# A SwiGLU layer on one core: one weight sum by an accumulating transfer, and six of seven products of 17 blocks with hi and lo side by side

## The chip, the core and the metric

The kernel runs on one core of a Trainium2 chip. The metric is the device time of one execution in microseconds (us). A core has a matrix engine (PE), whose weight loads appear in the profile as a lane of their own (PEld), a vector engine (DVE), a scalar engine (ACT), a general engine (POOL) and a queue engine (SP). Each works through its own list of instructions, and they wait for each other by semaphores. Transfers are issued by SP and POOL here and carried by 16 DMA engines.

## What is computed

The reference is one layer of a decoder with three sublayers and a final norm. The change touches only the first matrix product of the third one:

```python
    hf = rms_norm(x, norm_ffn[l])
    gate, up = jnp.split(hf @ w_ffn_in[l], 2, axis=-1)
    x = x + (jax.nn.silu(gate) * up) @ w_ffn_out[l]
return rms_norm(x, norm_final)
```

`hf` is 512 x 1024, `w_ffn_in` 1024 x 5632 (2816 gate columns and 2816 up columns), all in float32.

## The kernel before

**Precision.** Every float32 operand is held as two reduced-precision tiles, hi (a cast, on ACT) and lo (the operand minus hi, on DVE). A product is then hi x hi + hi x lo + lo x hi, three matmuls.

**The gate and up products.** The 2816 hidden columns are worked in 22 blocks m of 128. For one block the two products (gate and up) on two halves of the tokens and two halves of the contraction are formed by a seven-product scheme: seven weight forms, seven token forms, products 0 to 6, each over four steps k of the contraction with 256 tokens. The four raw weight quarters of a block lie in HBM next to each other. What is made of them:

- `ws`: two sums, each by a plain load followed by an accumulating load from POOL (L862). It gives the forms of products 4 and 2 ("pair 1").
- `wg`: quarters 0 and 1. It gives forms 0 and 1 ("pair 0"). Then `sum_third` (L874, DVE) adds one of the sums into the first half of `wg`, which gives form 3 (`third_cast`).
- `a` (the "corner", its own buffer): quarter 3 is loaded into its first half by `load_corner` (L868, SP), and `sum_last` (L878, DVE) writes the sum of the two halves of `wg` into its second half. It gives forms 5 and 6 ("pair 2").

`pair_cast` casts 128x1024 on ACT (L887); `rest_of` subtracts on DVE (L1006). For the form of product 3 both are 128x512 (L895, L1006).

**Narrow and wide products.** Where the token form keeps hi and lo side by side in one tile, one matmul of 512 columns does hi x (hi, lo), and a second of 256 columns does lo x hi (L909, L917): "wide". Else there are three matmuls of 256 (L914): "narrow". Products 1, 2 and 6 are wide in all blocks, product 5 in blocks 5 to 18 (`WIDE`), products 0, 3 and 4 never. A wide product leaves its result in two halves of a PSUM bank that still have to be added.

**Reading the banks.** Products 0, 3, 4 and 5 of a block add up in one bank z, which is copied out after 0, 3 and 4 (ACT, L946, 128x256) before the next one adds to it. `joined_halves` (L936, L937) adds both halves of a wide bank to such a copy, in two DVE instructions of 128x256: for product 1, for product 2 (`second`) and for product 6. `evict` then multiplies the gate half by the norm factors (L960), applies silu on ACT (L962), and forms the hidden activations (L971 where product 5 is wide, L974, L974, and L978 in every second block).

**Order.** PE, ACT and DVE follow the program's order. In the steady part the products run as (m,3), (m,2), (m,4), (m+1,0), (m+1,1), (m,5), (m,6), and the table `todo` says after which product each cast, subtraction, sum and read is put on its engine. p and q in that table are the positions of the products of m and m+1. Of each named piece of work, the part on the reads comes first, then the pieces in the order of the calls of `at`. The order on SP and POOL is made by the scheduler.

Of the kernel before, what the change touches and what calls it, by code (L numbers as in the profile page):

```python
# [11 lines left out]
ALU = mybir.AluOpType  # L12
# [13 lines left out]
NF = HID // P  # L26
HS = S // 2
# [17 lines left out]
def hybrid_layer(ctx: ExitStack, tc: tile.TileContext, xT_d, memT_d, mem_d, cols_d, wv_d, win_d,  # L45
                 wbr_d, wmix_d, wmq_d, wmk_d, wmv_d, wmo_d, wfi_d, wfo_d, gfin_d, out):
    nc = tc.nc
# [16 lines left out]
    def nm(s):  # L64
        count[0] += 1
        return f"{s}{count[0]}"
# [4 lines left out]
    def tmp(s, cols=512):  # L71
        return tpool.tile([P, cols], F32, tag="t", name=nm(s), padded_shape=[P, 512])

    def f(ap):
        return ap.bitcast(F32)
# [160 lines left out]
    first = nc.scalar.dma_start(gcol, cols_d)  # L236
# [398 lines left out]
    for m in range(KD):  # L635
        sig = []
        for j in range(2):
            if (m, j) not in gates:
                gate(m, j)
            t = gates.pop((m, j))  # L640
# [20 lines left out]
    for m in range(KD):  # L661
# [9 lines left out]
        t = tmp("km", MEM)  # L671
# [27 lines left out]
    def forms_of(xe, xo):  # L699

        b11, b12, b21, b22 = xe[:, :HS], xe[:, HS:], xo[:, :HS], xo[:, HS:]
        c, d = f(unit("c1")), f(unit("c2"))
        n1, t3, n2, t4 = c[:, :HS], c[:, HS:], d[:, :HS], d[:, HS:]
        nc.vector.tensor_tensor(out=n1, in0=b11, in1=b12, op=ALU.subtract)
        nc.vector.tensor_tensor(out=t3, in0=b22, in1=b12, op=ALU.subtract)
        nc.vector.scalar_tensor_tensor(out=n2, in0=n1, scalar=-1.0, in1=b22, op0=ALU.mult,  # L708
                                       op1=ALU.subtract)
        nc.vector.scalar_tensor_tensor(out=t4, in0=n2, scalar=-1.0, in1=b21, op0=ALU.mult,  # L710
                                       op1=ALU.subtract)
        u = unit("xf")
        nc.scalar.copy(u[:, :HS], b11)
        nc.vector.tensor_tensor(out=u[:, HS:], in0=b11, in1=f(u[:, :HS]), op=ALU.subtract)
        a, b = slice(0, HS), slice(HS, S)

        def beside(src, s):
            both = unit(s)
            nc.scalar.copy(both[:, a], src)
            nc.vector.tensor_tensor(out=both[:, b], in0=src, in1=f(both[:, a]), op=ALU.subtract)  # L720
            return both[:, a], both[:, b], both

        first = beside(b21, "xo")
        second, fourth = beside(n1, "xc"), beside(t3, "xc")
        third, fifth = beside(n2, "xd"), beside(t4, "xd")
        last = beside(b22, "xo")
        return [(u[:, a], u[:, b]), first, second, third[:2], fourth[:2], fifth, last]

    def residual(w_dram, act, old, gain, pairs=False):

# [56 lines left out]
    for h in range(MH):  # L787
        q = q_next
        scs = []
        for t2 in range(2):  # L790
            ps = ztile("sc")
            scs.append(ps)
            for i in range(2):
                t = 2 * t2 + i
# [5 lines left out]
        for t2 in range(2):  # L800
# [6 lines left out]
                                           in1=r1s[:, 2 * t2:2 * t2 + 2], op0=ALU.mult,  # L807
# [3 lines left out]
            for i in range(2):  # L811
                t = 2 * t2 + i
# [5 lines left out]
            for i in range(2):  # L818
                nc.vector.tensor_scalar(out=pr[:, i * MEM:(i + 1) * MEM],
                                        in0=pr[:, i * MEM:(i + 1) * MEM],  # L820
# [22 lines left out]

    KP = KD // 2
    raws, corners = {}, {}

    def ffn_load(m):

# [15 lines left out]

    def load_corner(m):

        a22 = corners[m] = fpool.tile([P, 2, 512], F32, tag="w2", name=nm("a22"))
        i = nc.sync.dma_start(a22[:, 0, :], wfi_d[m][:, 3 * 512:])  # L868
        if m < 2:
            after(i, [loads[-6]])  # L870

    def sum_third(m, eng=nc.vector):
        wg, s13 = raws[m]
        eng.tensor_tensor(out=wg[:, 0, :], in0=s13[:, 1, :], in1=wg[:, 0, :], op=ALU.add)  # L874

    def sum_last(m, eng=nc.vector):
        wg = raws[m][0]
        eng.tensor_tensor(out=corners[m][:, 1, :], in0=wg[:, 0, :], in1=wg[:, 1, :], op=ALU.add)  # L878

    wforms = {}  # L880

    def pair_cast(m, which):

        raw = (*raws[m], corners[m])[which]
        hi = wpool.tile([P, 2, 512], F32R, tag="wh", name=nm("wf"))
        lo = wpool.tile([P, 2, 512], F32R, tag="wl", name=nm("wf"))
        nc.scalar.copy(hi, raw)  # L887
        for n, i in enumerate(((0, 1), (4, 2), (5, 6))[which]):
            wforms[m, i] = hi[:, n, :], lo[:, n, :]
        return raw, hi, lo  # L890
# [11 lines left out]
    def product(ps, m, i, ks=range(KP)):  # L902

        rests = []
        for k in ks:
            hi, lo = (w[:, k * P:(k + 1) * P] for w in wforms[m, i])
            xh, xl, *both = x2f[k][i]
            if both and (i != 5 or m in WIDE):
                nc.tensor.matmul(ps, hi, both[0], start=i < 3 and k == 0, stop=False,  # L909
                                 skip_group_check=True)  # L910
                rests.append((ps[:, :HS], lo, xh))
                continue
            for j, (a, b) in enumerate(((hi, xh), (hi, xl), (lo, xh))):
                nc.tensor.matmul(ps[:, :HS], a, b, start=i < 3 and k == 0 and j == 0,  # L914
                                 stop=k == KP - 1 and j == 2, skip_group_check=True)
        for operands in rests:
            nc.tensor.matmul(*operands, start=False,  # L917
                             stop=ks[-1] == KP - 1 and operands is rests[-1],
                             skip_group_check=True)

    WIDE = range(5, NF - 3)
    banks, silus = {}, []
    acts = {}

# [10 lines left out]
    def joined_halves(out_, bank, old):  # L935
        nc.vector.tensor_tensor(out=out_, in0=bank[:, :HS], in1=old, op=ALU.add)  # L936
        nc.vector.tensor_tensor(out=out_, in0=bank[:, HS:], in1=out_, op=ALU.add)  # L937

    def reads(m, i):

        b = banks[m]
        z, s, t = b["z"][:, :HS], b["s"], b["t"]
        if i == 5 and m in WIDE:
            nc.scalar.copy(s[:, :HS], b["z"][:, HS:])
        elif i in (0, 3, 4):
            nc.scalar.copy((s[:, :HS], None, None, s[:, HS:], t[:, :HS])[i], z)  # L946
        elif i == 1:
            joined_halves(b["g"][:, :HS], b["v"], s[:, :HS])
        elif i == 6:
            joined_halves(b["g"][:, HS:], b["y"], s[:, HS:])  # L950

    def second(m):
        b = banks[m]
        joined_halves(b["t"][:, HS:], b["y"], b["t"][:, :HS])

    def evict(m, part):
        b = banks[m]
        g = b["g"]
        if part == 0:
            nc.vector.tensor_tensor(out=g, in0=g, in1=r2b[0], op=ALU.mult)  # L960
        elif part == 1:
            silus.append(nc.scalar.activation(g, g, AF.Silu))  # L962
        else:
            j, odd = divmod(m, 2)
            if not odd:
                acts[j] = f(unit("a1")), f(unit("a2"))
            to = slice(odd * HS, (odd + 1) * HS)
            first = b["z"][:, :HS]
            if m in WIDE:
                first = b["s"][:, :HS]  # L970
                nc.vector.tensor_tensor(out=first, in0=b["z"][:, :HS], in1=first, op=ALU.add)  # L971
            for half, u in enumerate((first, b["t"][:, HS:])):
                sl = slice(half * HS, (half + 1) * HS)
                nc.vector.scalar_tensor_tensor(out=acts[j][half][:, to], in0=u, scalar=-1.0,  # L974
                                               in1=g[:, sl], op0=ALU.mult, op1=ALU.mult)
            if not odd:
                n1 = acts[j][1][:, :HS]
                nc.vector.tensor_tensor(out=n1, in0=acts[j][0][:, :HS], in1=n1, op=ALU.subtract)  # L978
# [5 lines left out]
    m = NF - 1  # L984
# [134 lines left out]
    def at(n, *some):  # L1119
        todo.setdefault(n, []).extend(some)  # L1120

    def made(n, cast, *args, late=1):

        parts = []
        at(n, lambda: parts.append(cast(*args)))
        at(n + late, lambda: rest_of(*parts[0]))
# [14 lines left out]
    for m in range(1, NF - 1):  # L1141
        p = {i: uses.index((m, i)) for i in range(2, 7)}
        q = {i: uses.index((m + 1, i)) for i in range(2)}
        if m > 1:
            at(p[3], lambda m=m: sum_third(m + 1))
            at(p[3], lambda m=m: evict(m - 1, 0))
            at(p[2], lambda m=m: evict(m - 1, 1))
            at(q[0], lambda m=m: evict(m - 1, 2))
            made(p[3], pair_cast, m, 2)
            made(p[2], third_cast, m + 1)  # L1150
        else:
            made(p[4], third_cast, m + 1)
        at(p[4], lambda m=m: second(m))
        if m + 2 < NF:
            at(p[4], lambda m=m: load_corner(m + 2))
        made(q[0], pair_cast, m + 1, 1, late=2)
        at(q[1] if m < NF - 2 else p[4], lambda m=m: sum_last(m + 1))
        if m + 2 < NF:
            made(p[5], pair_cast, m + 2, 0)
    at(uses.index((0, 4)), lambda: second(0))  # L1160
# [33 lines left out]
    with tc.manual_schedule(engines={mybir.EngineType.PE, mybir.EngineType.Activation,  # L1194
# [69 lines left out]
        last = NJ - 2, NJ - 1  # L1264
# [17 lines left out]
        u = [plus("u", res[3][s2], s0[s2]) for s2 in range(2)]  # L1282
# [252 lines left out]
```

## Time and profile before

| | us |
|---|---|
| median of 3 runs | 839.92 (839.05 to 839.99) |
| the profiled execution, its own time | 838.75 |
| its span, first to last instruction | 837.0 |
| PE busy | 828.8 |
| VectorE busy | 684.6 |
| ScalarE busy | 463.9 |
| GpSimd busy | 161.2 |

The gate and up products stand from about 530 to 721 us of the span, and the down projection follows. Busy times are of single engines and overlap. A row of the timeline has the start in us, the time it took in us, the engine, the line, the operation and the tiles (written <- read). An instruction's start to the next one's start can be shorter than the time it took, since the end of one overlaps the start of the next. "x12" means that 12 like instructions in a row are merged. "[0.62 <-DVE fg L960]" says that the engine stood idle for 0.62 us before it and what ended that.

### The profile page before, as it was taken

What the parts mean: (1) busy time and instruction counts of PE and PEld (TensorE: products, weight loads), DVE (VectorE), ACT (ScalarE), POOL (GpSimd) and SP (SyncE); (2) the same over time, 40 slices, a digit from 0 to 9 for tenths busy, and PEclk for the clock granted to TensorE, in tenths of its full rate; (3) what the DMA queues carried; (4) which work ended last, traced back from release to release, by engine and by line L of the source; (5) the groups of instructions that cost most, each with busy time, mean ns of one, the idle gap of its engine ahead of it and who ended that gap; (6) DMA issues with size and microseconds to landing.
All of it is one profiled execution on the core that took longest, in us unless ns stands there. A gap on an engine that the chain in (4) does not pass through costs nothing.

```text
span 837.0 us, 11962 instructions
## 1 busy us (share of the span) xinstructions
PE 828.8 (99%) x4374; PEld 714.1 (85%) x4374; DVE 684.6 (82%) x1086; ACT 463.9 (55%) x796; POOL 161.2 (19%) x168
## 2 busy tenths in 40 slices
PE   9999999999999999999999999999999999999996
PEld 7888888888888888888888789999999999888885
DVE  7879899996756576587555698999999999999886
ACT  7567868674332355434444566645555555576654
POOL 0011131110566630173000031111111110000401
PEclk9999999999999999999999999999999999999999
DMA  8552435235687865566431326677767673465552
GB/s 303 155 166 101 122 111 103 74 115 174 228 312 276 304 249 188 182 233 249 148 82 51 101 51 161 167 184 200 197 180 197 176 184 95 170 213 197 180 183 101
DMA packets 51357, 143.69 MB, mean 172 GB/s; under 512 B 5761, under 2 KB 7041, under 8 KB 48482
## 3 DMA queue, kind: packets, MB, share of 16 engines
q1 hardware_dynamic: 41650, 107.89, 38.2%
q0 software_dynamic: 9360, 34.75, 15.8%
q8 instruction: 34, 0.56, 0.3%
q10 hardware_dynamic: 288, 0.28, 0.1%
q14 instruction: 25, 0.20, 0.1%
HBM read 125.20 MB, written 13.64 MB: 166 GB/s over the span
## 4 chain that ended last, share of the span: by engine, by line
PE 99%; DVE 0%; ACT 0%; DVEq 0%; issue 0%
PE z L914 13%; PE p L1228 12%; PE pr L161 8%; PE pr L162 8%; PE pr L163 8%; PE y L909 5%; PE r L162 3%; PE r L163 3%; PE r L161 3%; PE v L288 3%; PE y L917 2%; PE v L909 2%; PE km L666 2%; PE mq L163 2%; PE mq L161 2%; PE mq L162 2%
## 5 line engine op out<-in xcount | busy, mean ns | idle before, releaser
L156 ACT CAST wh<-wr 128x1024 fp32r<-128x1024 f32 x84 | 88.0, 1051 | 144.2 <-issue 80.0
L157 DVE TENSOR_TENSOR wl<-wr,wh 128x1024 fp32r<-128x1024 f32 x84 | 111.0, 1321 | 32.0 <-ACT wh L156 31.9
L161 PE MATMUL pr<-xgh,wh 128*128 128x512 f32 x288 | 112.8, 392 | 0.0
L162 PE MATMUL pr<-xgl,wh 128*128 128x512 f32 x288 | 112.4, 390 | 0.0
L163 PE MATMUL pr<-xgh,wl 128*128 128x512 f32 x288 | 112.3, 390 | 0.0
L611 POOL TENSOR_TENSOR pre<-pre 128x512 f32<-128x512 f32 x44 | 70.9, 1616 | 31.5 <-DMA pre<-in_w_ffn_out_dram 29.2
L862 POOL DMA_DIRECT2D ws<-in_w_ffn_in_dram x22 | 26.6, 1209 | 248.5 <-DVE c L708 54.0
L163 PEld LDWEIGHTS pr<-xgh,wl 128*128 128x128 f32 x288 | 54.1, 188 | 11.5
L161 PEld LDWEIGHTS pr<-xgh,wh 128*128 128x128 f32 x288 | 54.1, 188 | 10.6
L162 PEld LDWEIGHTS pr<-xgl,wh 128*128 128x128 f32 x288 | 54.1, 188 | 10.5
L914 PE MATMUL z<-xd,wf 128*128 128x256 f32 x360 | 47.5, 282 | 0.0
L946 ACT COPY sa<-z 128x256 f32<-128x256 f32 x44 | 16.4, 373 | 51.9 <-PE z L914 51.9
L914 PEld LDWEIGHTS z<-xd,wf 128*128 128x128 f32 x360 | 45.0, 190 | 0.1
L1006 DVE TENSOR_TENSOR wf<-wg,wf 128x1024 fp32r<-128x1024 f32 (+1 forms) x44 | 43.1, 978 | 1.5
L1006 DVE TENSOR_TENSOR wl<-wr,wh 128x1024 fp32r<-128x1024 f32 x33 | 41.0, 1242 | 1.8 <-ACT wh L1073 1.8
L1073 ACT CAST wh<-wr 128x1024 fp32r<-128x1024 f32 x33 | 34.5, 1050 | 5.3 <-ACT f01h L1002 2.6
L914 PE MATMUL z<-xf,wf 128*128 128x256 f32 x264 | 35.4, 283 | 0.0
L914 PE MATMUL z<-xc,wf 128*128 128x256 f32 x264 | 35.1, 283 | 0.0
L914 PEld LDWEIGHTS z<-xf,wf 128*128 128x128 f32 x264 | 33.4, 192 | 0.1
L914 PEld LDWEIGHTS z<-xc,wf 128*128 128x128 f32 x264 | 33.0, 190 | 0.0
L368 DVE TENSOR_TENSOR g<-pr,r0b 128x512 f32<-128x512 f32 x16 | 11.0, 687 | 23.5 <-PE pr L163 23.5
L417 POOL TENSOR_SCALAR_AFFINE_SELECT e<-e 128x128 f32<-128x128 f32 (+1 forms) x24 | 10.7, 447 | 86.6 <-DVE e L470 86.6
(356 smaller groups left out, 2239.9 us busy)
## 6 DMA issues: line engine op xcount, KB each, us to landing
wr<-in_w_in_dram SPq DMA_DIRECT2D x36, 512.0 KB, 3.4
pre<-in_w_ffn_out_dram POOLq DMA_DIRECT2D x11, 1024.0 KB, 8.0
sums<-pre POOLq DMA_DIRECT2D x11, 1024.0 KB, 5.0
ws<-in_w_ffn_in_dram SPq DMA_DIRECT2D x22, 512.0 KB, 4.8
wg<-in_w_ffn_in_dram SPq DMA_DIRECT2D x22, 512.0 KB, 4.7
ws<-in_w_ffn_in_dram POOLq DMA_DIRECT2D x22, 512.0 KB, 5.7
wr<-sums SPq DMA_DIRECT2D x22, 512.0 KB, 4.0
wr<-in_w_ffn_out_dram SPq DMA_DIRECT2D x16, 512.0 KB, 3.7
```

Source lines behind the costliest of these rows:

```text
L156: after(nc.scalar.copy(h2, raw), lead[-1:])
L157: lows.append(nc.vector.tensor_tensor(out=l2, in0=raw, in1=f(h2), op=ALU.subtract))
L161: nc.tensor.matmul(ps, a[0], b[0], start=start, stop=False, **kw)
L162: nc.tensor.matmul(ps, a[0], b[1], start=False, stop=False, **kw)
L163: nc.tensor.matmul(ps, a[1], b[0], start=False, stop=stop, **kw)
L611: nc.gpsimd.tensor_tensor(out=t[:, a, :], in0=t[:, a, :], in1=t[:, b, :], op=ALU.add)
L862: nc.gpsimd.dma_start(s13, a[:, 0:4:3, :], accum_op=ALU.add)
L909: nc.tensor.matmul(ps, hi, both[0], start=i < 3 and k == 0, stop=False, skip_group_check=True)
L914: nc.tensor.matmul(ps[:, :HS], a, b, start=i < 3 and k == 0 and j == 0, stop=k == KP - 1 and j == 2, skip_group_check=True)
L1006: nc.vector.tensor_tensor(out=lo, in0=src, in1=f(hi), op=ALU.subtract)
L1073: nc.scalar.copy(hi, raw)
L1228: nc.tensor.matmul(res[i][s2], a[:, ts], b, start=j == 0 and n == 0, stop=n == 2 and j == (BEHIND - 1 if (i, s2) == (5, 1) else NJ - 1))
```

## The change

Two ranges are set: `OWN` (blocks 3 to 20) for the weight sum, `WIDE` (now blocks 3 to 19) for the form of the products.

In the blocks of `OWN` the sum of the two halves of `wg` is made in place by an accumulating transfer from POOL (SBUF to SBUF) in place of the DVE instruction. Quarter 3 is then loaded over the first half of `wg` once form 3 has been cast and subtracted from it, and pair 2 is cast from `wg`. Its cast moves from after product 3 to after product 4, and its subtraction from after product 2 to after product (m+1,0).

In the blocks of `WIDE` products 3 and 4 become wide beside 5. The bank z is then copied whole (128x512) after 3 and 4. `folded` takes the place of `joined_halves` for products 2 and 6: one addition of 128x512 from PSUM, and one of 128x256 that adds the halves in SBUF.

```diff
+    OWN = range(3, NF - 1)
...
     def load_corner(m):
 
+        if m in OWN:
+            nc.sync.dma_start(raws[m][0][:, 0, :], wfi_d[m][:, 3 * 512:])
+            return
...
     def sum_last(m, eng=nc.vector):
         wg = raws[m][0]
+        if m in OWN:
+            nc.gpsimd.dma_start(wg[:, 1, :], wg[:, 0, :], accum_op=ALU.add)
+            return
         eng.tensor_tensor(out=corners[m][:, 1, :], in0=wg[:, 0, :], in1=wg[:, 1, :], op=ALU.add)
...
-        raw = (*raws[m], corners[m])[which]
+        raw = (*raws[m], raws[m][0] if m in OWN else corners[m])[which]
...
-            if both and (i != 5 or m in WIDE):
+            if both and (i not in (3, 4, 5) or m in WIDE):
...
-    WIDE = range(5, NF - 3)
+    WIDE = range(3, NF - 2)
...
-        if i == 5 and m in WIDE:
-            nc.scalar.copy(s[:, :HS], b["z"][:, HS:])
+        if m in WIDE and i in (3, 4):
+            nc.scalar.copy((s, t)[i - 3], b["z"])
+        elif m in WIDE and i == 5:
+            nc.scalar.copy(t[:, :HS], b["z"][:, HS:])
+        elif m in WIDE and i == 6:
+            folded(b["g"][:, HS:], b["y"], s)
...
+    def folded(out_, bank, old):
+        nc.vector.tensor_tensor(out=old, in0=bank, in1=old, op=ALU.add)
+        nc.vector.tensor_tensor(out=out_, in0=old[:, :HS], in1=old[:, HS:], op=ALU.add)
+
     def second(m):
         b = banks[m]
+        if m in WIDE:
+            folded(b["t"][:, HS:], b["y"], b["t"])
+            return
...
             if m in WIDE:
-                first = b["s"][:, :HS]
+                first = b["t"][:, :HS]
...
             at(p[3], lambda m=m: sum_third(m + 1))
+            if m + 1 in OWN:
+                at(p[3], lambda m=m: sum_last(m + 1))
+                at(p[5], lambda m=m: load_corner(m + 1))
             at(p[3], lambda m=m: evict(m - 1, 0))
...
-            made(p[3], pair_cast, m, 2)
+            made(p[4] if m in OWN else p[3], pair_cast, m, 2)
             made(p[2], third_cast, m + 1)
...
-        if m + 2 < NF:
+        if m + 2 < NF and m + 2 not in OWN:
             at(p[4], lambda m=m: load_corner(m + 2))
         made(q[0], pair_cast, m + 1, 1, late=2)
-        at(q[1] if m < NF - 2 else p[4], lambda m=m: sum_last(m + 1))
+        if m + 1 not in OWN:
+            at(q[1] if m < NF - 2 else p[4], lambda m=m: sum_last(m + 1))
```

The token forms of products 3 and 4 are now handed over with their joint tile as well (`third`, `fourth` in place of `third[:2]`, `fourth[:2]`).

Three places show how the instructions now stand. The first is VectorE in one steady block, from the read of the bank of product 6 to the first read of the next product 1. fg is the gate result, sa and sb are copies of the bank z, wf a hi or lo weight tile, a the corner (and, at L974, the activations). Before:

```order
L936 TENSOR_TENSOR fg_6062<-y_6121,sa_6040 128x256
L937 TENSOR_TENSOR fg_6062<-y_6121,fg_6062 128x256
L1006 TENSOR_TENSOR wf_6206<-wg_6075,wf_6205 128x1024
L874 TENSOR_TENSOR wg_6075<-ws_6073,wg_6075 128x512
L960 TENSOR_TENSOR fg_6062<-fg_6062,r0b_4940 128x512
L1006 TENSOR_TENSOR wf_6235<-a_6037,wf_6234 128x1024
L1006 TENSOR_TENSOR wf_6248<-wg_6075,wf_6248 128x512
L936 TENSOR_TENSOR sb_6154<-y_6237,sb_6154 128x256
L937 TENSOR_TENSOR sb_6154<-y_6237,sb_6154 128x256
L971 TENSOR_TENSOR sa_6040<-z_6039,sa_6040 128x256
```

The same place on VectorE in the changed kernel (L1024 is its subtraction, L964 and L965 are `folded`, L878 is `sum_third`, L978 the factor, L989 and L992 the eviction):

```order
L964 TENSOR_TENSOR sa_6064<-y_6143,sa_6064 128x512
L965 TENSOR_TENSOR fg_6090<-sa_6064 128x256
L1024 TENSOR_TENSOR wf_6222<-wg_6103,wf_6221 128x1024
L878 TENSOR_TENSOR wg_6103<-ws_6101,wg_6103 128x512
L978 TENSOR_TENSOR fg_6090<-fg_6090,r0b_4940 128x512
L1024 TENSOR_TENSOR wf_6257<-wg_6103,wf_6257 128x512
L964 TENSOR_TENSOR sb_6172<-y_6247,sb_6172 128x512
L965 TENSOR_TENSOR sb_6172<-sb_6172 128x256
L989 TENSOR_TENSOR sb_6065<-z_6063,sb_6065 128x256
```

The subtraction of pair 2 (128x1024, from a) no longer stands between the factor and the subtraction of form 3 (128x512, from wg); it comes behind the eviction.

The second place is ScalarE in a steady block, from the copy after product 3 to the copy after product 4. Before:

```order
L946 COPY sa_5811<-z_5810 128x256
L887 CAST wf_5889<-a_5692 128x1024
L962 ACTIVATE fg_5720<-fg_5720 128x512
L895 CAST wf_5903<-wg_5733 128x512
L946 COPY sb_5812<-z_5810 128x256
```

ScalarE in the changed kernel, from the copy after product 3 on:

```order
L951 COPY sa_5853<-z_5852 128x512
L980 ACTIVATE fg_5772<-fg_5772 128x512
L902 CAST wf_5942<-wg_5785 128x512
L951 COPY sb_5854<-z_5852 128x512
L894 CAST wf_5953<-wg_5681 128x1024
```

The cast of pair 2 (128x1024) moved from ahead of the silu to behind the copy after product 4; silu, cast of form 3 and that copy keep their order.

The third place is the SP queue in the steady part. Before, each corner has a buffer of its own:

```order
L857 DMA wg_6075<-in_w_ffn_in_dram 128x1024
L853 DMA ws_6073<-in_w_ffn_in_dram 128x2x512
L868 DMA a_6037<-in_w_ffn_in_dram 128x512
L857 DMA wg_6191<-in_w_ffn_in_dram 128x1024
L853 DMA ws_6189<-in_w_ffn_in_dram 128x2x512
```

SP in the changed kernel, where L869 is the load of the corner over the first half of `wg`:

```order
L869 DMA wg_5892<-in_w_ffn_in_dram 128x512
L858 DMA wg_6103<-in_w_ffn_in_dram 128x1024
L854 DMA ws_6205<-in_w_ffn_in_dram 128x2x512
L869 DMA wg_5996<-in_w_ffn_in_dram 128x512
L858 DMA wg_6207<-in_w_ffn_in_dram 128x1024
```

The corner's load now stands ahead of the load of the next `wg`, and on POOL one accumulating transfer of `wg` (L883) stands between each two of `ws` (L863).

More of the change, by code (lines that the diff above doesn't have):

```diff
@@ L726, in forms_of @@
         last = beside(b22, "xo")
-        return [(u[:, a], u[:, b]), first, second, third[:2], fourth[:2], fifth, last]
+        return [(u[:, a], u[:, b]), first, second, third, fourth, fifth, last]
     def residual(w_dram, act, old, gain, pairs=False):
```

## Prediction

> **What bounds the kernel now.** I read the page's busy times, the chain that ended last, and who PE waited for.
>
> ```profile
> PE 828.8 (99%) x4374; PEld 714.1 (85%) x4374; DVE 684.6 (82%) x1086; ACT 463.9 (55%) x796; POOL 161.2 (19%) x168
> PE 99%; DVE 0%; ACT 0%; DVEq 0%; issue 0%
> PE warm L248 <- DVE neg L92: 1.4, 1, 1.4
> ```
>
> PE is the whole chain, and its one wait of 1.4 us is at the start. So any instruction taken from PE shortens the end, as long as nothing else becomes late. Then busy time in a stretch of the gate and up products, where the change lies:
>
> ```profile
> core 0: us, PE busy (x) PEld busy (x) DVE busy (x) ACT busy (x) POOL busy (x), PEclk, DMA share, GB/s
> 610.00:620.00 10.00, 10.00 (x71) 9.30 (x71) 9.69 (x17) 5.49 (x10) 1.20 (x1) 1.00 0.71 185
> ```
>
> VectorE is at 9.69 of 10 us. The page's 82% hides this: here VectorE is almost as full as PE, so its order of work decides whether PE is fed. The chain in order of time prices the products (start, us, what):
>
> ```profile
> 612.23 0.93 PE z L909 x4
> 613.16 0.48 PE z L917 x4
> 613.63 0.93 PE y L909 x4
> 614.57 0.47 PE y L917 x4
> 615.03 1.43 PE z L914 x12
> ...
> 617.87 2.87 PE z L914 x24
> ...
> 622.14 0.93 PE z L909 x4
> ```
>
> A narrow product is 2.87/2 = 1.435 us, a wide one 0.93 + 0.48 = 1.41. From product 5 of one block (612.23) to product 5 of the next (622.14) is 9.91 us: one block.
>
> Last, the timeline of block 11, which holds every term of what follows.
>
> ```profile
> 613.78 1.22 DVE L1006 TENSOR_TENSOR wf<-ws,wf 128x1024 fp32r<-128x1024 f32 x1
> ...
> 614.87 1.59 PE L914 MATMUL z<-xd,wf 128*128 128x256 f32 x12
> 615.07 0.42 DVE L936 TENSOR_TENSOR fg<-y,sa 128x256 f32<-128x256 f32 x1
> ...
> 615.53 0.42 DVE L937 TENSOR_TENSOR fg<-y,fg 128x256 f32<-128x256 f32 x1
> 615.87 1.22 DVE L1006 TENSOR_TENSOR wf<-wg,wf 128x1024 fp32r<-128x1024 f32 x1
> ...
> 617.12 0.70 DVE L874 TENSOR_TENSOR wg<-ws,wg 128x512 f32<-128x512 f32 x1
> ...
> 617.73 0.69 DVE L960 TENSOR_TENSOR fg<-fg,r0b 128x512 f32<-128x512 f32 x1
> 618.33 1.22 DVE L1006 TENSOR_TENSOR wf<-a,wf 128x1024 fp32r<-128x1024 f32 x1
> 618.45 0.64 ACT L962 ACTIVATE fg<-fg 128x512 f32<-128x512 f32 x1 [0.62 <-DVE fg L960]
> 618.99 0.60 ACT L895 CAST wf<-wg 128x512 fp32r<-128x512 f32 x1
> ...
> 619.63 0.69 DVE L1006 TENSOR_TENSOR wf<-wg,wf 128x512 fp32r<-128x512 f32 x1
> 620.24 0.42 DVE L936 TENSOR_TENSOR sb<-y,sb 128x256 f32<-128x256 f32 x1
> ...
> 621.03 0.41 DVE L971 TENSOR_TENSOR sa<-z,sa 128x256 f32<-128x256 f32 x1
> 621.47 0.42 DVE L974 SCALAR_TENSOR_TENSOR a<-sa,fg 128x256 f32<-128x256 f32 x1
> 621.82 0.42 DVE L974 SCALAR_TENSOR_TENSOR a<-sb,fg 128x256 f32<-128x256 f32 x1
> 622.27 0.42 DVE L978 TENSOR_TENSOR a<-a,a 128x256 f32<-128x256 f32 x1
> 622.61 0.42 DVE L936 TENSOR_TENSOR fg<-v,sa 128x256 f32<-128x256 f32 x1
> ...
> 622.91 0.64 PE L917 MATMUL z<-xd,wf 128*128 128x256 f32 x4
> 623.40 0.68 DVE L878 TENSOR_TENSOR a<-wg 128x512 f32<-128x512 f32 x1
> 624.00 1.22 DVE L1006 TENSOR_TENSOR wf<-ws,wf 128x1024 fp32r<-128x1024 f32 x1
> ```
>
> The reader should see a latency that is covered. The factor (L960, 617.73) releases the silu (618.45). Behind the silu on ScalarE stands the cast of form 3 (618.99), and VectorE's subtraction of form 3 waits for that cast (619.63). From L960 to that subtraction it is 1.90 us, of which L960 itself holds VectorE for 0.60 (617.73 to 618.33). The other 1.30 us are filled by the subtraction of pair 2 (618.33).
>
> **The change part by part.**
>
> *PE.* 34 products (3 and 4 in 17 blocks) and product 5 in three more blocks become wide: 37 x (1.435 - 1.41) = 0.9 us less, where PE stays the bound.
>
> *Read-outs on VectorE.* `folded` is one addition of 128x512 with a PSUM source, then one of 128x256. The nearest row with a PSUM source:
>
> ```profile
> L368 DVE TENSOR_TENSOR g<-pr,r0b 128x512 f32<-128x512 f32 x16 | 11.0, 687 | 23.5 <-PE pr L163 23.5
> ```
>
> It takes 0.69 us, and a dependent instruction starts some 0.03 later (615.87 + 1.22 = 617.09 against 617.12): 0.72, then 0.34 (615.53 to 615.87), together 1.06. Now the pair takes 0.80 (615.07 to 615.87). So each of the two read-outs costs 0.26 more. The bounds for the 128x512 are 0.60 (start to start where nothing depends, 617.73 to 618.33) and 0.75; I take 0.72, since the second addition does depend.
>
> [...] L936 and L937 with a PSUM source and L978 with none all take 0.42 us. [...]
>
> *`sum_last` off VectorE.* 0.60 us per block saved (623.40 to 624.00). With two read-outs at +0.26, VectorE's pure work stays about level: -0.08.
>
> *Pair 2 moved, the term that decides.* Its subtraction goes behind the eviction. Nothing takes its place after the factor, and the queue is worked in order, so VectorE stands still for the 1.30 us between L960's slot and the cast of form 3, in every block. That is more than all its slack. How little that is, an earlier block shows, where VectorE ran 0.2 us behind PE:
>
> ```profile
> 604.18 1.22 DVE L1006 TENSOR_TENSOR wf<-ws,wf 128x1024 fp32r<-128x1024 f32 x1
> ...
> 605.31 0.42 DVE L936 TENSOR_TENSOR fg<-y,sa 128x256 f32<-128x256 f32 x1
> ```
>
> Here the subtraction holds VectorE for 1.13 us. In block 11 it would have been free at 613.78 + 1.13 = 614.91, and it read product 6 at 615.07: 0.16 us of slack. What is late next is pair 2's lo. Product 5 needs it at its second half (622.91); now it is done at 618.33 + 1.22 = 619.55, 3.36 us ahead. After the change it comes behind the read-out of product 2 and the eviction, and PE waits for it. Queued behind the waiting subtraction on VectorE are `second`, the eviction, pair 2, product 1's read-out, pair 1.
>
> The loop, from VectorE's first read of product 6 to the next one:
>
> - read-out 1.06; pair 0 1.25 (615.87 to 617.12); `sum_third` 0.61
> - factor to form 3, now bare: 1.90; form 3 0.61 (619.63 to 620.24)
> - `second` 1.06; eviction 621.03 to 622.61 1.58 with L978 (odd blocks), 0.45 less without
> - pair 2's subtraction to its end 1.22, and 0.03 to PE
> - second half of product 5 0.48, product 6 0.93 + 0.47, and 0.20 to VectorE (614.87 to 615.07)
>
> The sum is 11.40 us in odd blocks and 10.95 in even ones, against 9.91 now. VectorE's own stream alone, with pair 2 at 1.13, product 1's read-out 0.79 (622.61 to 623.40) and pair 1 1.14 in place of the last two lines, gives 11.14 and 10.69: the path through PE is the longer one, but both exceed the 9.86 (9.91 - 2 x 0.025) that PE needs.
>
> Blocks 3 to 19: 9 x 11.40 + 8 x 10.95 = 190.2, less 0.26 and 0.45 in block 3, whose first read-out and eviction belong to the narrow block 2: 189.5. Before, 17 x 9.91 = 168.5. That is **+21.0 us**. PE's 0.9 us is within it, not beside it.
>
> Block 20 keeps narrow products and `sum_last` of block 21 on VectorE, but pair 2 is late there too: 0.20 + 1.06 + 1.25 + 0.61 + 1.90 + 0.61 + 0.80 + 0.60 + 1.13 + 1.22 = 9.38 after the block's start, and the narrow product 5 needs it at 3 x 1.435 + 2 x 1.41 + 0.24 = 7.37: **+2.0**. Behind it PE never waits in the trace of before, so nothing gives this back.
>
> *ScalarE.* Two copies grow from 0.37 to about 0.62. They lie beside PE: the first ends before the silu is released; the second and pair 2's cast are done, by the same sums, 6.5 us into the block, and VectorE reaches pair 2 at 8.3. If that cover went, the loop would grow by the 1.06 of the cast at most. Cost 0.
>
> *Transfers.*
>
> ```profile
> ws<-in_w_ffn_in_dram POOLq DMA_DIRECT2D x14, 512.0 KB, 5.7
> wg<-in_w_ffn_in_dram SPq DMA_DIRECT2D x13, 512.0 KB, 4.6
> a<-in_w_ffn_in_dram SPq DMA_DIRECT2D x14, 256.0 KB, 2.6
> ```
>
> An SBUF to SBUF accumulation of 256 KB isn't in the trace: between 2.6 us (the plain load of that size) and 5.7 (the accumulating load of twice the size). I take 5.7, the nearest in kind. `sum_third` ends about 3.2 us into a block; the sum has landed by 8.9, the corner behind it by 11.5 to 13.5. Its cast comes 5.4 us into the next block, at 16.6: some 3 us of cover. On SP the load of the next `wg` is held behind the corner and behind the late release of its buffer (9.4), so it lands about 14; its cast is due a block later. POOL's queue is 1.2 us busy in ten. Cost 0.
>
> The sum: 838.75 (profiled) + 21.0 + 2.0 = 861.8. The median of before is 1.2 above that profiled execution; I state 862.
>
> **The rivals.**
>
> *PE stays the bound* (the other side). VectorE would have to hide the 1.30 us: only if its loop came under 9.86, so if at most some 0.15 us of it stood bare. For it: ScalarE is only half busy. Against it: the silu cannot start before L960 ends, and both are in the new order next to each other. It gives 838.75 - 0.9 = 837.8.
>
> *VectorE's stream alone bounds*, PE's lag not adding: 9 x 11.14 + 8 x 10.69 - 0.7 - 168.5 = +16.6, with block 20 at 0 to 2: 855 to 857. For it: the lo might arrive ahead through short waits I rounded up.
>
> *The accumulating transfer becomes the loop*: sum, corner, cast, pair 2, product 6 and round again spans two blocks. It decides once sum and corner take over 14 us together, against 8.3 to 10.4 by the rows. At twice the rows each block would be some 3 us longer: about 910. DMA engines stand at 0.71 busy already, which is all that speaks for it.
>
> *PE slows down after its new stalls*. The only stall in the trace is at the start, and the matmuls behind it took longer than the same shape later:
>
> ```profile
> L248 PE MATMUL warm<-neg 128*128 128x512 f32 x8 | 3.7, 641 | 1.4 <-DVE neg L92 1.4
> ```
>
> 3.7/8 = 0.46 us each against 0.93/4 = 0.23 in the chain. If one product after each stall ran at half rate, 17 x 1.4 = 24 us more: 886. Against it: the new stalls (about 1.4 us) are short beside a block. [...]
>
> **How the numbers follow.** The forecast (loop through PE) 0.83, 858 to 867; VectorE's stream alone 0.07; PE stays the bound 0.05; the transfer loop 0.03; the slower clock 0.02. The two ends of the 128x512 price move the sum by 34 x -0.12 = -4 and 34 x +0.03 = +1. The range takes these, the second rival and some waits that I missed: 854 to 869. A change of 0.2% (1.7 us) is about what a measurement can tell from none. Faster beyond that 0.02, within it 0.03 (the -0.9 falls there), slower 0.95.
>
> **What would show it.** Right: the subtraction of form 3 on VectorE has some 1.3 us of idle time before it, released by the cast; PE waits once per block, at the L924 matmuls of product 5, for VectorE's pair 2; blocks alternate between about 11 and 11.4 us; the granted clock stays 1.00; wide products still take 1.41. Wrong: PE without waits, or waits of ScalarE's pair 2 cast for the corner, which would make it the transfers.

## The result and the profile after

| | before | after |
|---|---|---|
| median, us | 839.64 (839.05 to 839.99, 5 runs) | 865.91 (864.72 to 866.48, 5 runs) |
| profiled execution, us | 838.75 | 866.17 |
| its span, us | 837.0 | 864.5 |

The changed kernel takes 1.0311 times as long, with an interval of 1.0296 to 1.0326. The prediction was 862, with 854 to 869.

These are lines of the page of the changed kernel: busy times, then the shares of the chain that ended last.

```profile
PE 834.4 (97%) x4226; PEld 706.4 (82%) x4226; DVE 684.2 (79%) x1071; ACT 470.9 (54%) x799; POOL 177.1 (20%) x186
PE 78%; DVE 17%; ACT 3%; issue 2%; DVEq 0%
```

VectorE is as busy as before (684.2 us against 684.6), yet it now holds 17% of the chain, where it had none. So it does not work more; others wait for it at another place. Who waits for whom stands in the view of the waits (us in total, times, the longest), first PE's, then one row of VectorE's:

```profile
PE z L924 <- DVE wf L1024: 19.8, 17, 1.4
PE z L921 <- DVE wf L1024: 1.9, 1, 1.9
PE warm L248 <- DVE neg L92: 1.4, 1, 1.4
...
DVE wf L1024 <- ACT wf L902: 21.8, 18, 1.2
```

PE waits 17 times at the L924 matmuls of product 5 and once at L921, where block 20's product 5 is still narrow. VectorE waits 18 times for the cast of form 3, once per block of `OWN`. Both are the waits that the prediction named. The timeline of one steady block shows how the second makes the first:

```profile
625.91 0.69 DVE L964 TENSOR_TENSOR sa<-y,sa 128x512 f32<-128x512 f32 x1 [0.31 <-PE y L924]
626.63 0.42 DVE L965 TENSOR_TENSOR fg<-sa 128x256 f32<-128x256 f32 x1
626.98 1.22 DVE L1024 TENSOR_TENSOR wf<-wg,wf 128x1024 fp32r<-128x1024 f32 x1
...
628.23 0.69 DVE L878 TENSOR_TENSOR wg<-ws,wg 128x512 f32<-128x512 f32 x1
...
628.84 0.68 DVE L978 TENSOR_TENSOR fg<-fg,r0b 128x512 f32<-128x512 f32 x1
...
629.56 0.63 ACT L980 ACTIVATE fg<-fg 128x512 f32<-128x512 f32 x1 [1.66 <-DVE fg L978]
...
630.10 0.60 ACT L902 CAST wf<-wg 128x512 fp32r<-128x512 f32 x1
...
630.73 0.69 DVE L1024 TENSOR_TENSOR wf<-wg,wf 128x512 fp32r<-128x512 f32 x1 [1.21 <-ACT wf L902]
...
633.99 1.22 DVE L1024 TENSOR_TENSOR wf<-wg,wf 128x1024 fp32r<-128x1024 f32 x1
...
635.26 0.74 PE L924 MATMUL z<-xd,wf 128*128 128x256 f32 x4 [1.41 <-DVE wf L1024]
...
635.84 1.09 PE L916 MATMUL y<-xo,wf 128*128 128x512 f32 x4
...
637.44 0.69 DVE L964 TENSOR_TENSOR sa<-y,sa 128x512 f32<-128x512 f32 x1 [0.31 <-PE y L924]
```

From the factor (628.84) over the silu and the cast to the subtraction of form 3 (630.73) it is 1.89 us, and VectorE stands idle for 1.21 of it. Pair 2's subtraction so begins at 633.99, PE gets its lo at 635.26 after 1.41 us of waiting, and VectorE in turn waits for product 6 (637.44). From one read of product 6 to the next it is 11.53 us.

The extra 27.5 us of span lie here (starts of matmuls in the two timelines; the product named is the one with which the stretch begins or ends):

| stretch | before | after | more | predicted |
|---|---|---|---|---|
| to product 3 of block 3 | 535.51 | 535.76 | 0.25 | 0 |
| from there to product 3 of block 20 | 168.61 | 191.93 | 23.3 | 21.0 |
| from there to the down projection | 17.04 | 20.75 | 3.7 | 2.0 |
| to the end of the span | 115.84 | 116.06 | 0.2 | 0 |

The third row holds something that was not in the forecast. A row of PE's timeline in block 20:

```profile
737.11 4.07 PE L921 MATMUL z<-xd,wf 128*128 128x256 f32 x22 [1.92 <-DVE wf L1024]
```

And the windows around it (from:to, length, busy time and count of PE, PEld, DVE, ACT, POOL, then the granted clock, the DMA share, GB/s):

```profile
737.00:738.00 1.00, 0.89 (x7) 0.89 (x8) 0.97 (x4) 0.01 (x1) 0.00 (x0) 1.00 0.59 221
738.00:739.00 1.00, 1.00 (x8) 1.00 (x7) 1.00 (x2) 0.00 (x0) 0.00 (x0) 0.68 0.01 4
739.00:740.00 1.00, 1.00 (x7) 1.00 (x6) 1.00 (x1) 0.00 (x0) 0.00 (x0) 0.50 0.01 4
740.00:741.00 1.00, 1.00 (x7) 1.00 (x7) 1.00 (x2) 0.00 (x0) 0.00 (x0) 0.50 0.85 270
741.00:742.00 1.00, 1.00 (x4) 0.83 (x4) 0.26 (x1) 0.78 (x2) 0.00 (x0) 0.61 0.64 229
742.00:743.00 1.00, 1.00 (x9) 0.92 (x9) 0.85 (x2) 0.94 (x3) 0.00 (x0) 1.00 0.37 78
```

The wait is 1.92 us, as forecast (2.0). Behind it the granted clock falls to a half: 0.32 + 0.50 + 0.50 + 0.39 = 1.71 us of full clock are missing, which is 3.42 us at half clock.

### The profile page after: what moved, and what is told of

The parts are those of the page before. It is cut to its first block, busy times and chain, and to the rows that moved or that the text cites. A ratio compares the mean times of both kernels' runs of the same rounds, so it can differ in the third digit from the quotient of the medians.

```text
span 864.5 us, 11703 instructions
## 1 busy us (share of the span) xinstructions
PE 834.4 (97%) x4226; PEld 706.4 (82%) x4226; DVE 684.2 (79%) x1071; ACT 470.9 (54%) x799; POOL 177.1 (20%) x186
## 4 chain that ended last, share of the span: by engine, by line
PE 78%; DVE 17%; ACT 3%; issue 2%; DVEq 0%
PE p L1250 12%; PE pr L161 8%; PE pr L162 8%; PE pr L163 8%; DVE wf L1024 7%; PE r L162 3%; PE r L163 3%; PE r L161 3%; PE v L288 3%; PE y L916 2%; PE km L666 2%; PE mq L162 2%; PE mq L163 2%; PE mq L161 2%; PE br L161 2%
## 5 line engine op out<-in xcount | busy, mean ns | idle before, releaser
L1024 DVE TENSOR_TENSOR wf<-wg,wf 128x1024 fp32r<-128x1024 f32 (+1 forms) x62 | 65.1, 1049 | 21.9 <-ACT wf L902 21.8
L863 POOL DMA_DIRECT2D ws<-in_w_ffn_in_dram x22 | 27.1, 1231 | 134.5 <-DVE c L707 52.6
L1024 DVE TENSOR_TENSOR wl<-wr,wh 128x1024 fp32r<-128x1024 f32 x33 | 40.5, 1228 | 3.8 <-ACT wh L1091 3.8
L894 ACT CAST wf<-wg 128x1024 fp32r<-128x1024 f32 x40 | 42.1, 1053 | 2.3 <-PE r L162 1.8
L883 POOL DMA_DIRECT2D wg<-wg x18 | 16.6, 925 | 128.6 <-DVE wg L878 80.8
L924 PEld LDWEIGHTS z<-xd,wf 128*128 128x128 f32 x136 | 19.6, 189 | 28.5 <-DVE wf L1024 27.1
L924 PE MATMUL z<-xd,wf 128*128 128x256 f32 x136 | 23.5, 295 | 19.8 <-DVE wf L1024 19.8
L916 PE MATMUL z<-xd,wf 128*128 128x512 f32 x136 | 37.2, 395 | 0.0
L921 PE MATMUL z<-xf,wf 128*128 128x256 f32 x264 | 35.4, 283 | 0.0
L980 ACT ACTIVATE fg<-fg 128x512 f32<-128x512 f32 x22 | 13.9, 633 | 37.1 <-DVE fg L978 37.0
L921 PEld LDWEIGHTS z<-xf,wf 128*128 128x128 f32 x264 | 33.3, 192 | 0.1
```

What stands on the lines that cost most here:

```text
L924: nc.tensor.matmul(*operands, start=False, stop=ks[-1] == KP - 1 and operands is rests[-1], skip_group_check=True)
L1024: nc.vector.tensor_tensor(out=lo, in0=src, in1=f(hi), op=ALU.subtract)
```

## The experiments

My theory: the whole loss is the bare wait before form 3 plus two dearer read-outs, both on a VectorE that had 0.16 us of room in a block. The rivals: the wide products and their read-outs alone; the transfers; the clock. Eight kernels tell them apart. The medians of the kernel before beside them were 839.67 (7 runs, for the first four told here) and 839.23 (9 runs, for the others).

### The sum and pair 2 alone

The kernel before with only the part on `OWN`: the accumulating transfer, the corner over `wg`, pair 2 late. Products and read-outs stay as they were.

```diff
+    OWN = range(3, NF - 1)
...
+            if m + 1 in OWN:
+                at(p[3], lambda m=m: sum_last(m + 1))
+                at(p[5], lambda m=m: load_corner(m + 1))
...
-            made(p[3], pair_cast, m, 2)
+            made(p[4] if m in OWN else p[3], pair_cast, m, 2)
```

> The weight sum by the accumulating transfer with pair 2 moved behind product 4, but products 3 and 4 narrow and product 5 wide in blocks 5 to 18 only, as before the change. Theory (the move of pair 2's subtraction lays 1.30 us of waiting for the cast of form 3 bare on VectorE): the loop through product 5 is 0.5 us shorter than in the changed kernel, since both read-outs are the old pairs of 0.80 us: 10.54 us in even and 11.00 in odd blocks, +15 us over blocks 3 to 19 and some 2 to 4 at block 20: 856 to 859. Rival (the wide products and their longer read-outs cost the time): within 2 us of before, 839 to 841.

Measured: 862.35 (862.03 to 863.81, 4 runs), 1.0276 times before (1.0259 to 1.0293). The steady loops were 10.53 and 10.98 us, as forecast; the total (856 to 859) was not. One block took 15.24 us. A row of ScalarE's waits:

```profile
ACT wf L894 <- DMA wg<-in_w_ffn_in_dram: 7.0, 3, 4.7
```

And one of PE's timeline in that block:

```profile
580.77 1.97 PE L916 MATMUL z<-xd,wf 128*128 128x512 f32 x4 [3.52 <-ACT wf L894]
```

The cast of pair 2 waited three times for the corner's transfer, the longest time 4.7 us, and there PE waited 3.52 us for the cast. The four matmuls behind it took 1.97 us in place of 1.09: in the windows from 581 to 584 us the granted clock was 0.50. Why this corner came late, VectorE's `sum_third` and POOL's queue show:

```profile
561.29 0.70 DVE L878 TENSOR_TENSOR wg<-ws,wg 128x512 f32<-128x512 f32 x1
...
569.85 1.20 POOL L863 DMA_DIRECT2D ws<-in_w_ffn_in_dram  x1 [11.66 <-DMA ws<-in_w_ffn_in_dram]
570.56 1.43 POOL L883 DMA_DIRECT2D wg<-wg  x1
```

The input of the sum was ready at 561.99, but the sum was issued at 570.56 only, behind the accumulating load of `ws`, which stood 11.66 us until the transfer that it adds to had landed. The corner's load comes behind the sum and was issued at 577.01. In the steady block of the changed kernel shown above the sum was issued 0.54 us after its input was ready (628.92, 629.46). What follows: the bare wait carries most of the loss, and the 3 us of cover that I had worked out for the transfers can go where a wait in POOL's queue holds up the sum.

### The wide products alone

The changed kernel with `OWN` empty.

```diff
-    OWN = range(3, NF - 1)
+    OWN = range(0)
```

> Products 3, 4 and 5 wide in blocks 3 to 19 with the new read-outs, but the weight sum on VectorE, the corner in its own buffer and pair 2 cast behind product 3, as before the change. Theory: VectorE has 0.52 us more to do per block and no bare wait; its stream (about 10.2 in even, 10.6 in odd blocks) passes PE's 9.86 once its lead is used up after some blocks: +4 to +7 us, 844 to 847. Rival (wide read-outs cost the time): about as slow as the changed kernel, 860 or more. Rival (VectorE has room): PE's saving, 838.7.

Measured: 847.02 (846.57 to 847.14, 4 runs), ratio 1.0087 (1.0072 to 1.0102): at the upper end of the forecast. VectorE's timeline gives the price of a read-out:

```profile
640.36 0.68 DVE L964 TENSOR_TENSOR sa<-y,sa 128x512 f32<-128x512 f32 x1
641.07 0.42 DVE L965 TENSOR_TENSOR fg<-sa 128x256 f32<-128x256 f32 x1
641.42 1.22 DVE L1024 TENSOR_TENSOR wf<-wg,wf 128x1024 fp32r<-128x1024 f32 x1
```

From 640.36 to 641.42 it is 1.06 us, the forecast to the hundredth, against 0.80 before. From one read of product 6 to the next it is 10.14 and 10.60 us in turn: PE's shorter products (9.86) don't show, since VectorE, which had 0.16 us of room, got 0.52 more to do.

### The silu behind the cast of form 3

The changed kernel with two steps in the other order, so that the cast no longer stands behind the silu.

```diff
-            at(p[2], lambda m=m: evict(m - 1, 1))
...
             made(p[2], third_cast, m + 1)
+            at(p[2], lambda m=m: evict(m - 1, 1))
```

> The changed kernel with the cast of form 3 ahead of the silu on ScalarE, nothing else. Theory: form 3's cast no longer waits for the factor and the silu, only for the sum of wg, so VectorE's bare wait shrinks by 0.57 us per block (loops of 10.51 and 10.97 us): 17 x 0.57 = 9.6 us less than the changed kernel, 854 to 857. Rival (VectorE's wait is made by something else, the transfers or PE): no change, 864 to 867.

Measured: 854.19 (853.74 to 856.18, 4 runs), ratio 1.0178 (1.0163 to 1.0193), as forecast. Loops of 10.48 and 10.92, 0.60 shorter than after. Its timeline at the same place:

```profile
625.01 0.68 DVE L978 TENSOR_TENSOR fg<-fg,r0b 128x512 f32<-128x512 f32 x1
625.13 0.62 ACT L902 CAST wf<-wg 128x512 fp32r<-128x512 f32 x1 [1.05 <-DVE wg L878]
...
625.79 0.69 DVE L1024 TENSOR_TENSOR wf<-wg,wf 128x512 fp32r<-128x512 f32 x1
...
626.92 0.69 DVE L964 TENSOR_TENSOR sb<-y,sb 128x512 f32<-128x512 f32 x1 [0.44 <-ACT sb L951]
```

From factor to subtraction it is 0.78 us in place of 1.89. Of the gain, 0.44 us goes back one step later, where `folded` waits for the copy that now stands behind the silu. So the bare wait is the chain factor, silu, cast: with the silu behind the cast, the wait and the loops became shorter. The longest wait of PE here was 1.2 us, and behind none of its waits did four matmuls of 512 columns take more than 1.11 us.

### Pair 2 where it was

The changed kernel with pair 2 cast and subtracted at its old place, the accumulating transfer kept.

```diff
-            made(p[4] if m in OWN else p[3], pair_cast, m, 2)
+            made(p[3], pair_cast, m, 2)
```

> The changed kernel with one thing undone: pair 2 is cast behind product 3 and subtracted behind product 2 again, still from the tile that the accumulating transfer and the corner's load fill. Theory: the subtraction covers the wait for form 3 again, VectorE's stream is 9.8 us on average, PE bounds at 9.86 per block: 0.9 to 1.1 us faster than before, 838.4 to 838.9, if the corner lands 10.1 us into the block before, as in the changed kernel, and its cast is due at 11.9. Rival (the transfers are what the move made room for, and now land too late): ScalarE's cast of pair 2 waits for a transfer in each block, 845 or more. Rival (the cost is in the transfers or the read-outs, not in the order): 860 or more.

Measured: 850.21 (849.57 to 850.38, 4 runs), ratio 1.0124 (1.0109 to 1.0140). My forecast missed and the rival, late transfers, was right. One row of ScalarE's waits:

```profile
ACT wf L894 <- DMA wg<-in_w_ffn_in_dram: 44.7, 17, 3.8
```

The landings of the two new kinds of transfer in the view of the transfers (KB each, median us from issue to landing), in this kernel:

```profile
wg<-wg POOLq DMA_DIRECT2D x18, 256.0 KB, 3.5
wg<-in_w_ffn_in_dram SPq DMA_DIRECT2D x18, 256.0 KB, 5.8
```

The same rows in the changed kernel:

```profile
wg<-wg POOLq DMA_DIRECT2D x18, 256.0 KB, 3.4
wg<-in_w_ffn_in_dram SPq DMA_DIRECT2D x18, 256.0 KB, 4.3
```

The bare wait is gone: blocks that nothing holds up take 9.86 us, just what PE needs. But the cast of pair 2 now comes before the corner has landed, in 17 blocks, and the blocks in which this reaches PE take 10.1 to 11.5. The accumulation lands in 3.4 to 3.5 us, well under the 5.7 I took; the corner behind it takes 4.3 to 5.8, where the median of all 22 corners in the kernel before was 3.0 by the same view. So the two edits of the change hang together as they are built here: the sum by transfer with the corner behind it needs pair 2 later, and pair 2 later lays the wait bare. Other work of VectorE in the gap was not tried.

### The sum into a buffer of its own

Here the transfer accumulates into the corner's buffer, whose two quarters are loaded early (a second load of quarter 1, 256 KB more from memory in each block), so that no load stands behind the sum; pair 2 is at its old place.

```diff
     def load_corner(m):
-        if m in OWN:
-            nc.sync.dma_start(raws[m][0][:, 0, :], wfi_d[m][:, 3 * 512:])
-            return
         a22 = corners[m] = fpool.tile([P, 2, 512], F32, tag="w2", name=nm("a22"))
+        if m in OWN:
+            nc.sync.dma_start(a22[:, 1, :], wfi_d[m][:, 512:2 * 512])
...
-            nc.gpsimd.dma_start(wg[:, 1, :], wg[:, 0, :], accum_op=ALU.add)
+            nc.gpsimd.dma_start(corners[m][:, 1, :], wg[:, 0, :], accum_op=ALU.add)
```

> The changed kernel with the accumulating transfer writing into the corner's own buffer: quarters 3 and 1 are loaded there early (256 KB per block more from HBM), the first half of wg is added by the transfer after the sum for form 3, and pair 2 is cast behind product 3 as before the change. No load has to wait for form 3 and the sum. Theory: the sum lands about 8 us into a block, its cast is due at 11.9, VectorE is covered again, PE bounds at 9.86: 838.5 to 840. Rival (the DMA engines, at 0.88 busy already with pair 2 back, are the limit): loads land late, 845 or more.

Measured: 849.81 (848.19 to 850.01, 4 runs), ratio 1.0121 (1.0108 to 1.0135). The forecast missed again, and the time is the rival's. A row of ScalarE's waits and one of POOL's:

```profile
ACT wf L893 <- DMA a<-wg: 26.5, 9, 4.2
...
POOL ws L863 <- DMA ws<-in_w_ffn_in_dram: 39.2, 7, 11.5
```

And the landing of the sum:

```profile
a<-wg POOLq DMA_DIRECT2D x18, 256.0 KB, 6.5
```

The sum now is late itself. On POOL the accumulating load of `ws` stands ahead of the sum, and it waits up to 11.5 us for the transfer that it adds to. In seven of the 18 blocks the sum was issued directly behind that load, 2.4 to 8.0 us after its input was ready, and then took 6.3 to 9.0 us to land; these are seven of the nine late casts. For the other two the sum was issued within 0.9 us, but landed after 8.0 and 7.6. So the queue held the sum, and its transfer was slower too (median 6.5 us, against 3.4 in the changed kernel), as the rival had it: from 649 to 655 us the DMA share was 0.95 to 1.10. How much each adds, no run separates. A buffer of its own for the sum did not help here. One stall of PE in this kernel matters for the clock, further below; from its timeline:

```profile
650.20 1.20 PE L915 MATMUL z<-xd,wf 128*128 128x512 f32 x4 [1.78 <-ACT sb L950]
```

The four matmuls behind 1.78 us of waiting take 1.20 us, not 1.97 as above, and the granted clock stays at 1.00 (windows from 649 to 655 us).

### The sum on GpSimd

The wide products as above, `OWN` empty, and the sum computed by GpSimd ahead of its deadline.

```diff
-    OWN = range(3, NF - 1)
+    OWN = range(0)
+    POOLED = range(3, NF - 1)
...
+            if m + 1 in POOLED:
+                at(p[3], lambda m=m: sum_last(m + 1, nc.gpsimd))
```

> Products 3, 4 and 5 wide in blocks 3 to 19 as in the changed kernel; the weight sum of blocks 3 to 20 is an addition on GpSimd into the corner's own buffer, right behind the sum for form 3, and pair 2 is cast behind product 3 as before. Theory: the transfer chain and the bare wait are both gone, VectorE has 0.6 us less to do per block than in e2_wide_only, its stream is about 9.8 us on average and PE bounds at 9.86: 838.5 to 839.5. Rival (GpSimd's addition comes late behind its waits for transfers, or slows VectorE's own additions): VectorE or ScalarE waits, 842 to 850.

Measured: 857.69 (857.05 to 858.63, 4 runs), ratio 1.0220 (1.0207 to 1.0234), some 11 us worse than the wide products with the sum on VectorE. A wide miss, and outside the rival's range too. Its timeline in two blocks; in the second GpSimd's addition comes later, beside another instruction:

```profile
629.14 1.61 POOL L886 TENSOR_TENSOR a<-wg 128x512 f32<-128x512 f32 x1 [6.02 <-DVE wg L879]
...
629.51 2.32 DVE L1025 TENSOR_TENSOR wf<-a,wf 128x1024 fp32r<-128x1024 f32 x1
...
640.45 1.22 DVE L1025 TENSOR_TENSOR wf<-a,wf 128x1024 fp32r<-128x1024 f32 x1
...
642.53 1.78 POOL L886 TENSOR_TENSOR a<-wg 128x512 f32<-128x512 f32 x1
...
643.07 1.55 DVE L966 TENSOR_TENSOR sb<-sb 128x256 f32<-128x256 f32 x1
```

The same subtraction takes 2.32 us beside GpSimd's addition and 1.22 without: it ends 1.08 us after GpSimd does (631.83 against 629.14 + 1.61 = 630.75), roughly as if it had begun only then. In the second block the addition of 128x256 beside GpSimd takes 1.55 us, and 0.42 in the block before (633.07). What was taken off VectorE (0.60) came back larger: 1.10 us in the first block, 1.13 in the second. By what GpSimd's addition holds VectorE up, no run shows.

### Block 20 left out

The changed kernel with `OWN` one block shorter, so that the narrow block 20 keeps its old order.

```diff
-    OWN = range(3, NF - 1)
+    OWN = range(3, NF - 2)
```

> The changed kernel without block 20 in the range of the accumulating transfer (blocks 3 to 19 instead of 3 to 20), nothing else. It tells what PE's longest stall (1.92 us at product 5 of block 20, with the granted clock at 0.50 for 3.4 us behind it in the profile) is worth. If the slow clock follows that stall and costs half of 3.4 us: 1.9 + 1.7 = 3.6 us less than the changed kernel, 861 to 863, and the granted clock is 1.00 there. If the clock has nothing to do with the stall: 1.9 less, 864 to 865, with a stretch of 0.50 still there.

Measured: 863.93 (862.58 to 865.69, 5 runs), ratio 1.0298 (1.0284 to 1.0312). The profiled run took 862.58 us, its span is 3.6 us below that of after, and the granted clock was 1.00 through block 20 (windows from 725 to 745 us): by the profile, the stall of 1.92 and the 1.7 behind it went together. The medians differ by 2.0 only, about the stall alone (1.6 when each is taken against the kernel before beside it); 863.93 lies between the two forecasts, and the five runs spread over 3.1 us, the longest at a mean clock of 0.996 and the shortest at 0.999. Only one run of this kernel has a profile, so whether the others had a slow stretch at another place stays open.

### Stalls of several lengths

The kernel before, with additions of 128x128 on VectorE that serve no result (0.32 us each) ahead of pair 2's subtraction: 3 to 12 of them, in seven blocks.

```diff
+    DELAYS = {5: 11, 7: 3, 9: 5, 11: 6, 13: 7, 15: 9, 17: 12}
+
+    def delay(m):
+        for _ in range(DELAYS.get(m, 0)):
+            nc.vector.tensor_tensor(out=neg_f, in0=neg_f, in1=neg_f, op=ALU.add)
...
+            at(p[2], lambda m=m: delay(m))
```

> The kernel before with additions of 128x128 to a scratch tile put on VectorE ahead of pair 2's subtraction: 11 in block 5 (uses up the lead), then 3, 5, 6, 7, 9 and 12 in blocks 7, 9, 11, 13, 15 and 17. It measures the granted clock against the length of PE's stall by itself. If a stall of some length lowers the clock: no stretch of 0.50 behind the short stalls (1 to 1.6 us), some behind those of 1.9 to 2.3, always behind those over 3, each 3.4 us long. If the clock in the changed kernel was something else: 1.00 everywhere. Time: 839 plus some 14 us of stalls, plus 1.7 for each slow stretch: 850 to 862.

Measured: 852.44 in one run. The stalls came out shorter than planned: only one is above 1 us. In the other blocks PE stood for up to 0.92 us at a time, and no four matmuls of 512 columns there took more than 1.19 us. In block 17 it stood for 1.92 and, after four matmuls, 0.66:

```profile
693.46 0.74 PE L922 MATMUL z<-xd,wf 128*128 128x256 f32 x4 [1.92 <-DVE wf L1011]
...
694.86 1.97 PE L914 MATMUL y<-xo,wf 128*128 128x512 f32 x4 [0.66 <-DVE sb L942]
```

From 695 to 698 us the granted clock was 0.50, and 0.79 in the next one: 1.71 us lost, as in block 20 and in the first experiment. So the drop came also without the accumulating sum and a corner that waits for it, behind stalls of PE (1.92 and 0.66 us) that VectorE alone had made.

None of these versions beats the kernel before.

## Why the prediction was right, point by point

**The bare wait.** Right in place and size: 1.89 us from factor to form 3 (forecast 1.90), 18 waits of about 1.2 us, shown as the cause by the reversed order, which took 0.60 per block away, and by pair 2 at its old place, where VectorE's waits for form 3 are gone.

**The read-outs.** Right: 1.06 us. The loop with them is 0.55 longer than without (11.53 against 10.98, first experiment), the forecast 0.52. The addition of 128x512 takes 0.72 from start to start, the value taken between the bounds.

**`sum_last` off VectorE.** Right: its 0.60 is no longer in the loop, and VectorE's busy time stayed level.

**The loop through PE.** The step that was mis-sized: "pair 2's subtraction to its end 1.22, and 0.03 to PE" and "second half of product 5 0.48". In the timeline PE starts 0.05 after the subtraction's end (633.99 + 1.22 = 635.21 against 635.26), and the half takes 0.58 (635.26 to 635.84): its four matmuls last 0.74 us in place of 0.64. The rows of the weight loads (PEld) beside it, first in the kernel before, then in the changed one:

```profile
612.77 0.65 PEld L917 LDWEIGHTS z<-xd,wf 128*128 128x128 f32 x4
613.00 0.64 PE L917 MATMUL z<-xd,wf 128*128 128x256 f32 x4
...
635.26 0.54 PEld L924 LDWEIGHTS z<-xd,wf 128*128 128x128 f32 x4 [1.84 <-DVE wf L1024]
635.26 0.74 PE L924 MATMUL z<-xd,wf 128*128 128x256 f32 x4 [1.41 <-DVE wf L1024]
```

The forecast took the price of a half whose weight load begins 0.23 us ahead of it, beside earlier matmuls; here the load begins only when the wait ends, together with the matmuls. It is not needed for this that PE waits for the weights. With pair 2 where it was, PE waited for a copy of the bank, with its hi cast at 595.36 already:

```profile
596.93 0.76 PEld L916 LDWEIGHTS z<-xd,wf 128*128 128x128 f32 x4 [1.51 <-ACT sb L951]
596.93 1.19 PE L916 MATMUL z<-xd,wf 128*128 128x512 f32 x4 [1.31 <-ACT sb L951]
```

Here too the load begins with the matmuls, and they take 1.19 us in place of 1.09. That the load is what the 0.1 us goes to is read from these rows; no run tells it from another cost of starting again. Both parts together are 0.12 a block, 17 x 0.12 = 2.0 of the 2.3 us by which this stretch was off. All other terms of the loop came within 0.02. Most of what is left is block 3, where VectorE began 0.49 us behind PE's product 3 (535.76, 536.25) and the sum had 0.20.

**Block 20.** The lateness was right (1.92 against 2.0). What the sum left out is the clock behind it, 1.7 us, and the sign "the granted clock stays 1.00" failed there. The prediction had a slower PE behind its stalls among the rivals, with 0.02, as a tax on 17 of them; it came once, behind the longest.

**ScalarE: 0.** Right, no wait in the changed kernel goes back to its longer copies or pair 2's cast.

**Transfers: 0.** Right for the changed kernel: sum and corner took 3.4 + 4.3 = 7.7 us by their medians, where the forecast had 8.3 to 10.4 (its rows add up to 10.3), and the cast waited for the corner once, 0.5 us. But the cover was thinner than "some 3 us": with pair 2 only one product earlier the corner is late in 17 blocks, and in the first experiment in three, by up to 4.7 us. What the prediction overlooked is that POOL's queue, "1.2 us busy in ten", also stands still while an accumulating load in it waits, for up to 11.7 us there.

**The rivals.** PE did not stay the bound, and the products' 0.9 us shows nowhere. VectorE's stream alone would have given 11.14 and 10.69 (its terms add up to 0.01 less); the loops are 11.53 and 11.08, through PE. The transfer loop decided in none of the blocks.

Sum of the misses on the profiled times: 866.17 - 861.8 = 4.4, of which 2.0 is the later start and the longer matmuls behind PE's waits, 1.7 the clock, 0.45 the start and the end of the stage (0.25 and 0.2, not followed up), and the rest small deviations of the loop.

## What to carry to other kernels

Before an instruction is moved on its engine, look at what its old place was covering: here the subtraction filled the 1.3 us in which two ScalarE steps had to run, and the bare wait of 1.21 us that it left is twice the 0.60 that the saved addition brought. Work taken off a full engine and given to a transfer or to another engine keeps its deadline, and its latency (3.4 us and a queue) or what it holds up beside it (1.10 us of a subtraction beside GpSimd's addition) can cost more than the 0.6 us that it took before. A queue that is 1.2 us busy in ten can still hold up a transfer, when the one ahead of it waits (POOL's, by up to 11.7 us in the first experiment). When a loop comes to run through a wait of PE, count what the matmuls behind the wait take longer too, 0.1 us here (0.74 in place of 0.64).

## What the hardware showed unexpectedly

- The granted clock fell to 0.50 for about 3.4 us (1.71 us lost each time) behind stalls of PE of 1.92 us (in two kernels; in one of them 0.66 more followed after four matmuls) and 3.52 us, beginning 0.15 to 1.5 us after PE had resumed. It did not fall behind the 17 stalls of up to 1.4 us in the changed kernel (1.00 from 536 to 730 us), nor behind one of 1.78 us in the kernel with the sum in its own buffer (1.00 from 649 to 655). Whether the length of the stall decides, or something else at that moment, was not tried.
- Beside an addition on GpSimd a subtraction on VectorE took 2.32 us, and 1.22 without one (the kernel with the sum on GpSimd, 629.51 and 640.45).
- An accumulating transfer of 256 KB within SBUF landed in 3.4 us in the changed kernel, 0.4 more than the plain load of that size from memory in the kernel before (3.0 by the same view), but in 6.5 where the sum had a buffer of its own (medians).
